# Decoder block on one core: a third column pair's first two MLP products moved to the entry of the stage, with one finished bank copied out of PSUM

## The chip, the cores and the metric

The kernel runs on one core of a Trainium2 chip. The metric is the device time of one execution, in microseconds; the time before is the median of three runs. The engines are named as in the profile: PE is TensorE's matmul, PEld its weight load, DVE is VectorE, ACT is ScalarE, POOL is GpSimd, SP is the engine that issues most of the DMAs.

## The reference

One decoder block over 1024 tokens of width 1024 in float32. Only its last part bears on the change:

```python
x = x + g1[:, None, :] * token_mixer(h, ...)          # retention + dilated attention
h = modulate(rms_norm(x, norm2_g[l]), sh2, sc2)
x = x + g2[:, None, :] * squared_relu_mlp(h, w_ff1[l], w_ff2[l])
return rms_norm(x, norm_f_g)

def squared_relu_mlp(h, w1, w2):
    return jnp.square(jax.nn.relu(h @ w1)) @ w2        # w1: 1024 x 4096, w2: 4096 x 1024
```

## The kernel before

Everything is kept transposed: 128 features on the partitions, tokens along the free dimension. Each float32 operand is split into a high part (`hi`, rounded to the format that PE multiplies) and a low part (`lo` = value minus `hi`), and each product is three matmuls, low weight by high data, high by low, high by high (`mm3`, L207, L209 and L211). The split takes two engines: ACT casts the `hi`, and then DVE subtracts to get the `lo`.

The first MLP product `h @ w1` is the function `ff1`. It works on one pair of 128-column blocks of `w1` at a time: `q` is the number of the pair, 0 to 15. For each pair the two columns by two halves of the tokens are computed with seven block products instead of eight (Winograd's form of Strassen's scheme). The products are named "11", "s1", "s3", "s2", "12", "22", "s4" (`ORDER`). Each is 4 contraction blocks of 3 matmuls of 128x512, that is 12 matmuls. "11" and "12" need only `h` of the first half of the tokens, "22" and "s4" need the second half or a sum of it, and "s1", "s3", "s2" need sums over both halves, which are called t1, t3 and t2 here (`OPERAND`).

The class `Blocks` holds the scheme. `prep` makes a weight operand: for the "s" products a DVE sum into a buffer shared by the pair (L249), then the ACT cast (L254), while the DVE subtraction for the low part (L264) is put off until the next `prep`, or until `flush` is called. `mm` issues the 12 matmuls. `post` combines finished banks on DVE and ACT. A pair has four PSUM banks: bank 0 collects "11" and then "12", bank 1 "s1" and later "s4", bank 2 "s2", bank 3 "s3" and later "22". So `post(q, "11")` copies bank 0 to SBUF before "12" is added to it (L286), and `post(q, "s2")` has DVE read bank 2 (L290) and bank 3 (L291) before "22" may be added to bank 3, and bank 1 (L1988) before "s4" may. `BANK` and `ORDER` put "12" between "s2" and "22". `run` goes through a list of items; after each product it issues the `prep` calls for which there are weight slots, then the `post`; for "s2" the `post` comes ahead of the `prep` calls. Every engine takes its instructions in the order in which this Python code issues them.

The entry of `ff1` is written out by hand. At its start the second half of the tokens isn't normalised yet: its sum of squares has just been finished by the stage before (`wo_step`). The entry runs "11" of pairs 0 and 1 around the row sums (L364) and the broadcast of the reciprocal root (L380, `n21rb`), then "12" of pairs 0 and 1. Meanwhile DVE normalises the second half (`norm`, L2038), makes t1 (L2056), t3 (L2070), t2 (L2079) and t4 (L2096), and `x_split` casts them on ACT (L2026, L2029) and subtracts on DVE (L2027, L2030). Then come "s1", "s3", "s2" of pairs 0 and 1 by hand, and `run` takes over with "s4" and "22" of both and then all products of pairs 2 to 15. There are eight PSUM banks of one tile each, so in the entry only two pairs have all their banks.

The queue of ACT in the entry is: copy of bank 0 of pair 0, copy of bank 0 of pair 1 (L286), the cast of pair 2's "s3" weight (L254), the four casts of t1, and so on. The queue of DVE is: the sums for pair 2's "s1" and "s3" weights with the low part of "s1", then the first `norm`.

`f_temps` gives the two SBUF temporaries of a pair in `post`, tags `nsq` and `h2t`, two buffers each; `norm_acc` shares `nsq` for its squares, in the stage before and in the last stage. `a_sums` makes and stores operand sums of the MLP's second product from finished pairs, at places set by `late`.

## Time and profile before

| | |
|---|---|
| median of three runs | 2219.44 us (2218.9 to 2220.44) |
| profiled execution, its own time | 2219.0 us |
| span of that execution in the profile | 2217.1 us |
| mean granted TensorE clock | 0.998 |
| PE busy | 2175.5 us, 98% of the span |
| DVE, ACT, POOL busy | 1458.5 us (66%), 919.4 us (41%), 160.8 us (7%) |
| `ff1` starts | 1569.56 us after the span's start |

A row of the timeline has the start in us from the span's start, the duration in us, engine, line of the kernel, operation, output and inputs by the program's names, and in brackets the idle time of the engine just before it with what ended it. Matmuls are pipelined: a row's duration is longer than the distance to the next one, so the pace of PE is read from the starts. A row of the waits has the total in us, how often, and the longest. A row of the windows has the length of the stretch, then the busy time and the number of instructions of each engine, then the granted clock, the DMA share and GB/s.

### The profile page before, as it was taken

What the parts mean: (1) busy time and instruction counts of PE and PEld (TensorE: products, weight loads), DVE (VectorE), ACT (ScalarE), POOL (GpSimd) and SP (SyncE); (2) the same over time, 40 slices, a digit from 0 to 9 for tenths busy, and PEclk for the clock granted to TensorE, in tenths of its full rate; (3) what the DMA queues carried; (4) which work ended last, traced back from release to release, by engine and by line L of the source; (5) the groups of instructions that cost most, each with busy time, mean ns of one, the idle gap of its engine ahead of it and who ended that gap; (6) DMA issues with size and microseconds to landing.
All of it is one profiled execution on the core that took longest, in us unless ns stands there. A gap on an engine that the chain in (4) does not pass through costs nothing. (4 is left out here: it accounts for less than half of the span.)

```text
span 2217.1 us, 27237 instructions
## 1 busy us (share of the span) xinstructions
PE 2175.5 (98%) x10130; PEld 1802.5 (81%) x10130; DVE 1458.5 (66%) x2289; ACT 919.4 (41%) x1681; POOL 160.8 (7%) x192
## 2 busy tenths in 40 slices
PE   7999999999999999999999999999999999999998
PEld 5888888888887888888888878888778888788887
DVE  6618777764548788865655654676876665787855
ACT  4323332223434544544644633524454445533412
POOL 0001111000012211111100000001100000000003
PEclk9999999999999999999999999999999999999999
DMA  9539999625775556557763265654144444745322
GB/s 365 201 133 285 298 287 287 199 105 180 249 270 185 184 189 199 178 183 196 168 173 97 68 238 190 237 179 161 65 155 154 148 147 183 253 135 173 121 86 77
DMA packets 156611, 408.93 MB, mean 184 GB/s; under 512 B 27446, under 2 KB 55357, under 8 KB 153278
## 3 DMA queue, kind: packets, MB, share of 16 engines
q1 hardware_dynamic: 148542, 363.14, 46.6%
q0 software_dynamic: 7936, 44.05, 9.0%
q8 instruction: 80, 1.31, 0.2%
q14 instruction: 53, 0.43, 0.1%
HBM read 316.27 MB, written 156.13 MB: 213 GB/s over the span
## 5 line engine op out<-in xcount | busy, mean ns | idle before, releaser
L207 PE MATMUL qap<-hh,qaw 128*128 128x512 f32 x216 | 84.0, 389 | 0.0
L209 PE MATMUL qap<-hl,qaw 128*128 128x512 f32 x216 | 84.0, 389 | 0.0
L211 PE MATMUL qap<-hh,qaw 128*128 128x512 f32 x216 | 84.0, 389 | 0.0
L631 POOL TENSOR_TENSOR j<-qk,j 128x512 fp32r<-128x512 f32 x32 | 43.3, 1352 | 459.8 <-ACT j L630 459.8
L1989 ACT ACTIVATE a<-a 128x512 f32<-128x512 f32 x48 | 30.3, 632 | 76.2 <-DVE a L1988 76.2
L1886 POOL TENSOR_TENSOR accnf<-accnf,sqnf 128x256 f32<-128x256 f32 (+1 forms) x18 | 16.6, 922 | 613.9 <-ACT sqnf L1885 613.9
L264 DVE TENSOR_TENSOR fw<-w1r,fw 128x512 fp32r<-128x512 f32 x48 | 33.0, 688 | 37.6 <-ACT fw L254 37.6
L1312 ACT ACTIVATE P<-P,ng 128x128 f32<-128x128 f32 (+1 forms) x96 | 41.9, 438 | 37.1 <-DVE ng L1309 37.1
L264 DVE TENSOR_TENSOR qaw<-wa,qaw 128x512 fp32r<-128x512 f32 x54 | 36.0, 686 | 30.8 <-ACT qaw L254 30.7
L2175 ACT CAST w2h<-w2s 128x512 fp32r<-128x512 f32 x36 | 22.4, 622 | 77.3 <-DVE w2s L2213 75.5
L207 PE MATMUL fp<-h2h,fw 128*128 128x512 f32 x128 | 50.0, 390 | 0.0
L211 PE MATMUL fp<-h2h,fw 128*128 128x512 f32 x128 | 49.8, 389 | 0.0
L207 PE MATMUL roa<-rh,rwl 128*128 128x512 f32 x128 | 49.8, 389 | 0.0
L209 PE MATMUL roa<-rl,rwh 128*128 128x512 f32 x128 | 49.8, 389 | 0.0
L211 PE MATMUL roa<-rh,rwh 128*128 128x512 f32 x128 | 49.8, 389 | 0.0
L209 PE MATMUL fp<-h2l,fw 128*128 128x512 f32 x128 | 49.8, 389 | 0.0
L1724 DVE TENSOR_TENSOR rwl<-rwl,rwh 128x1024 fp32r<-128x1024 f32 x25 | 30.2, 1220 | 29.0 <-ACT rwh L1754 29.0
L207 PEld LDWEIGHTS qap<-hh,qaw 128*128 128x128 f32 x216 | 40.5, 188 | 8.5
L666 ACT COPY sm<-sT 128x128 f32<-128x128 f32 x32 | 8.5, 267 | 93.8 <-PE sT L654 93.8
L211 PEld LDWEIGHTS qap<-hh,qaw 128*128 128x128 f32 x216 | 40.5, 188 | 8.4
L209 PEld LDWEIGHTS qap<-hl,qaw 128*128 128x128 f32 x216 | 40.5, 188 | 8.4
L1886 POOL TENSOR_TENSOR accn<-accn,sqn 128x512 f32<-128x512 f32 x12 | 15.5, 1296 | 399.9 <-ACT sqn L1885 399.9
(3097 smaller groups left out, 7210.9 us busy)
## 6 DMA issues: line engine op xcount, KB each, us to landing
v<-vd SPq DMA_DIRECT2D x32, 512.0 KB, 5.0
raw<-in_w_ada_dram SPq DMA_DIRECT2D x32, 512.0 KB, 5.0
w1r<-in_w_ff_dram SPq DMA_DIRECT2D x32, 512.0 KB, 5.0
vd<-vo SPq DMA_DIRECT2D x24, 512.0 KB, 6.3
yt<-y POOLq DMA_DIRECT2D x24, 512.0 KB, 7.3
xsd<-as SPq DMA_DIRECT2D x24, 512.0 KB, 2.8
w2r<-in_w_ff2s_dram SPq DMA_DIRECT2D x24, 512.0 KB, 7.1
em<-in_w_ada_dram SPq DMA_DIRECT2D x16, 512.0 KB, 10.2
```

Source lines behind the costliest of these rows:

```text
L207: nc.tensor.matmul(o, wl, xh, start=first, stop=False, skip_group_check=skip)
L209: nc.tensor.matmul(o, wh, xl, start=False, stop=False, skip_group_check=skip)
L211: nc.tensor.matmul(o, wh, xh, start=False, stop=last, skip_group_check=skip)
L264: nc.vector.tensor_sub(t[:, 512:], src, fv(t[:, :512]))
L631: nc.gpsimd.tensor_sub(t[:, 1], src, fv(t[:, 0]))
L666: nc.scalar.copy(sm, ps[:, :C])
L1312: nc.scalar.activation(v, v, AF.Exp, bias=ng[:, blk:blk + 1], accum_out=st[:, g, blk, 2 + a:3 + a])
L1724: nc.vector.tensor_sub(lo, fv(lo), fv(hi))
L1886: (nc.vector if f == 7 else nc.gpsimd).tensor_add(G["acc", key], G["acc", key], sq)
L1989: nc.scalar.activation(o, o, AF.Relu)
L2175: nc.scalar.copy(hi, src)
```

## The change

Pair 2's "11" now runs in the entry between "12" of pair 1 and "s1" of pair 0, with its `post`, and pair 2's "12" runs between "s1" of pair 1 and "s3" of pair 0. Both are taken out of the list that `run` gets, and `post(2, "12")` is issued after pair 2's "s3". For this, pair 2 needs a ninth bank: bank 0 of pair 0, finished after "12", is copied by ACT to a new SBUF tile `f11`, from which `post(0, "12")` reads later. The "12" weight of pair 2 is prepared in the entry too, directly behind the "s3" weight. The temporaries of `post` are given one at a time, the second only at "s2", and `nsq` has a third buffer. Two of the `a_sums` calls move to other items.

```diff
@@ Blocks.post
             if n == "11":
-                self.t[q] = self.temps(f"{self.name}t{q}")
+                self.t[q] = [self.temps(f"{self.name}t{q}", 0)]
                 nc.scalar.copy(self.t[q][0], a)
                 return
-            u, v = self.t[q]
+            if n == "s2":
+                self.t[q].append(self.temps(f"{self.name}t{q}", 1))
+            u, v = self.t[q][0], self.t[q][-1]
@@ norm_acc
-            sq = pool.tile([P, 512], F32, tag="nsq", bufs=2, name=f"sq{key}{f}")[:, :n]
+            sq = pool.tile([P, 512], F32, tag="nsq", bufs=3, name=f"sq{key}{f}")[:, :n]
@@
-    def f_temps(name):
-        return [G["mp"].tile([P, 512], F32, tag=t, bufs=2, name=name + t) for t in ("nsq", "h2t")]
+    def f_temps(name, i):
+        t = ("nsq", "h2t")[i]
+        return G["mp"].tile([P, 512], F32, tag=t, bufs=3 - i, name=name + t)
@@ ff1
         BF.mm(1, "11", range(2, 4))
         BF.post(1, "11")
-        BF.prep((2, "s3"))
+        BF.prep((2, "s3"), (2, "12"))
         BF.mm(0, "12")
+
+        t = G["mp"].tile([P, 512], F32, tag="f11", name="f11")
+        nc.scalar.copy(t, BF.ps[0][0])
+        BF.ps[0][0] = t
         BF.mm(1, "12")
...
         norm(1)
         low()
+        BF.mm(2, "11")
+        BF.post(2, "11")
         BF.mm(0, "s1")
         BF.mm(1, "s1")
+        BF.mm(2, "12")
...
-        sums = [(q, n) for q in range(2, NQ) for n in ORDER]
+        sums = [(q, n) for q in range(2, NQ) for n in ORDER if (q, n) not in ((2, "11"), (2, "12"))]
         items = [(q, n) for n in ("s4", "22") for q in range(2)] + sums
...
-        late = {(0, "22"): (0, 0), (2, "11"): (0, 1), (2, "12"): (1, 0), (2, "22"): (1, 1)}
+        late = {(0, "22"): (0, 0), (2, "s1"): (0, 1), (2, "s2"): (1, 0), (2, "22"): (1, 1)}
...
             if (q, n) in late:
                 a_sums(*late[q, n])
+            if (q, n) == (2, "s3"):
+                BF.post(2, "12")
...
-        BF.run(items, sums[3:], before, after, ("s2",))
+        BF.run(items, sums[2:], before, after, ("s2",))
```

The temporaries of the earlier scheme (`a_temps`, the attention and gate projections) follow the new form of `post` and give the same two halves of one tile as before.

More of the change, by code (lines that the diff above doesn't have):

```diff
@@ L944, in a_two, with a_temps @@
         return t.rearrange("p (a b) -> p a b", a=2)
-    def a_temps(name):
-        t = a_two(name)
-        return t[:, 0], t[:, 1]
+    pairs = {}
+    def a_temps(name, i):
+        if i == 0:
+            pairs[name] = a_two(name)
+        return pairs[name][:, i]
     def a_out(q, n, x, y=None):
```

## The prediction

> **What bounds the kernel now.** First the head of the page and the table of engines: is there one engine whose work is the span?

> ```profile
> span 2217.1 us, 27237 instructions
> PE 2175.5 (98%) x10130; PEld 1802.5 (81%) x10130; DVE 1458.5 (66%) x2289; ACT 919.4 (41%) x1681; POOL 160.8 (7%) x192
> ```

> PE is, and the change leaves the number of its matmuls as it is. It can win time only where PE waits, so the second view is PE's waits.

> ```profile
> PE n10rb L380 <- POOL n1rs L373: 8.2, 1, 8.2
> PE av L804 <- ACT hh L481: 3.6, 5, 1.2
> PE fp L209 <- DVE xt L2027: 3.6, 4, 1.1
> PE pc L418 <- DMA crow<-in_c_dram: 2.3, 1, 2.3
> PE ao L207 <- ACT g L1636: 1.8, 1, 1.8
> PE nf2ss L364 <- DVE accnf L1886: 1.6, 1, 1.6
> PE fp L207 <- DVE ft2h2t L291: 1.5, 1, 1.5
> ```

> The rows of `n10rb`, `av` and `pc` are the start of the kernel, `nf2ss` is its end. The rows of `fp` are the banks of the first MLP product: 3.6 us for low parts of t3 and t2, and 1.5 us once for a `post`. Together 5.1 us, 0.23% of the time, is all that a reordering here can take away. The rest of the argument is read from the timeline. 0.2% of 2219.44 us, 4.4 us, is about what a measurement of this kernel can tell from no change.

> First PE in the entry. A product is 12 matmuls; the first rows of products:

> ```profile
> 1580.54 0.39 PE L207 MATMUL fp<-h2h,fw 128*128 128x512 f32 x1
> ...
> 1583.26 0.39 PE L207 MATMUL fp<-xt10h,fw0s 128*128 128x512 f32 x1
> ...
> 1594.57 0.50 PE L209 MATMUL fp<-xt,fw0s 128*128 128x512 f32 x1 [1.09 <-DVE xt L2027]
> ...
> 1597.92 0.39 PE L207 MATMUL fp<-xt,fw0s 128*128 128x512 f32 x1
> ```

> These are the starts of "12" of pair 1 and "s1" of pair 0, the matmul in "s3" of pair 0 that waits last, and the start of "s2" of pair 0. A product without a wait takes 1583.26 - 1580.54 = 2.72 us. From 1583.26 to 1597.92 are four products, "s1" and "s3" of both pairs: 10.88 us of work in 14.66. The rest is "s3" of pair 0, whose matmuls come no faster than DVE makes t3. So in the entry DVE sets the pace, and the question is what the change does to DVE's queue and what to PE's.

> **The change part by part.**

> *The two products that move.* 2 x 2.72 = 5.44 us of PE work enter the stretch between "12" of pair 1 and "s3" of pair 0, and leave the run of pair 2 behind it. No matmul is added.

> *The weight for "12" of pair 2.* Its cast on ACT and its subtraction on DVE move from behind t4 to the entry. By that the subtraction for the "s3" weight moves too: `prep` flushes the one before it. In the built order of the changed kernel DVE has this subtraction directly ahead of the first `norm`, and it waits for the cast on ACT.

> ```profile
> 1573.83 0.68 DVE L249 TENSOR_TENSOR fs<-w1r,w1r 128x512 f32<-128x512 f32 x1
> ...
> 1576.64 0.75 DVE L2038 SCALAR_TENSOR_TENSOR x<-x,a,n21rb 128x512 f32<-128x512 f32 x1 [1.53 <-PE n21rb L380]
> ...
> 1579.73 0.70 DVE L2027 TENSOR_TENSOR xt10l<-x,xt10h 128x512 fp32r<-128x512 f32 x1 [0.24 <-ACT xt10h L2026]
> 1580.34 0.74 DVE L2038 SCALAR_TENSOR_TENSOR x<-x,a,n21rb 128x512 f32<-128x512 f32 x1
> ...
> 1584.97 0.69 DVE L2027 TENSOR_TENSOR xt13l<-x,xt13h 128x512 fp32r<-128x512 f32 x1
> 1585.58 0.75 DVE L2070 SCALAR_TENSOR_TENSOR x<-x,dsh,x 128x512 f32<-128x512 f32 x1
> ...
> 1578.07 0.59 ACT L286 COPY ft1nsq<-fp 128x512 f32<-128x512 f32 x1 [3.46 <-PE fp L211]
> 1578.56 0.62 ACT L254 CAST fw2s<-fs 128x512 fp32r<-128x512 f32 x1
> 1579.08 0.62 ACT L2026 CAST xt10h<-x 128x512 fp32r<-128x512 f32 x1
> ```

> The sum for "s3" is there at 1574.5 (1573.83 + 0.68), but the cast on ACT starts only at 1578.56, since ACT stands before it in the copy of pair 1's bank, which waits for PE to end that product. The cast ends at 1579.18. DVE, which starts `norm` at 1576.64 now, would be held until 1579.21 and be through at 1579.81 (a subtraction takes 0.61 from start to start, 1579.73 to 1580.34; I use 0.60): `norm` comes 3.17 us later, and behind it in DVE's queue stands everything that PE waits for: t1, t3, t2, t4. A little comes back: the 0.24 us for which t1's first subtraction waits (row 1579.73) is gone, and the cast that it waits for, which stands behind others now (1579.08), follows its sum at once; the rest of t1 is 2.85 us late. Then the flush of the "12" weight itself stands between t1 and t3 (ahead of row 1585.58), 0.60 more. **t3, t2 and t4 are 3.45 us late.**

> *The copy of the finished bank.* One ACT copy of 0.59 us (row 1578.07), behind the casts. It waits for the end of "12" of pair 0, about 1580.7, and stands ahead of t1's first cast, which now comes at 1579.08. By itself it would delay that to 1581.3; but t1's sum, 3.17 us late, ends at 1581.28. So it costs nothing, as long as DVE is the later one. The later activation reads SBUF instead of PSUM: taken as equal. The copy of pair 2's bank (0.59 us) falls in a gap of ACT before a cast that needs `norm`. The third `nsq` buffer and the two moved `a_sums` add no instruction.

> *PE in the entry.* "11" of pair 2 runs from 1583.26 to 1585.98; its weight is made ahead of all these rows already now. "s1" then finds t1's last low part at 1584.97 + 2.85 + 0.69 = 1588.51 and waits 0.3 us; both "s1" end at 1591.87, "12" of pair 2 at 1594.59. "s3" of pair 0 has no wait for its second and third block any more, but the last low part of t3, which released row 1594.57, comes 3.45 later: 1598.02. From there "s2" starts at 1597.92 + 3.45 = 1601.37. **At "s2" PE is 3.45 us late with 5.44 us of work done ahead: 1.99 us gained.** "s2" itself waits for t2 as before, 3.45 later, and so does what follows up to the end of "22" of pair 1.

> *What stands behind "s2" of pair 2.* Here is the loss. Rows of PE, then DVE:

> ```profile
> 1616.15 0.39 PE L207 MATMUL fp<-h2h,fw 128*128 128x512 f32 x1
> ...
> 1631.41 0.50 PE L207 MATMUL fp<-xt,fw 128*128 128x512 f32 x1 [1.50 <-DVE ft2h2t L291]
> ...
> 1611.06 0.69 DVE L249 TENSOR_TENSOR fs<-fs,w1r 128x512 f32<-128x512 f32 x1
> ...
> 1613.47 0.69 DVE L264 TENSOR_TENSOR fw2s<-fs,fw2s 128x512 fp32r<-128x512 f32 x1 [1.12 <-ACT fw2s L254]
> ...
> 1618.42 0.69 DVE L264 TENSOR_TENSOR fw<-w1r,fw 128x512 fp32r<-128x512 f32 x1 [2.46 <-ACT fw L254]
> ...
> 1622.38 0.69 DVE L264 TENSOR_TENSOR fw2s<-fs,fw2s 128x512 fp32r<-128x512 f32 x1 [0.74 <-ACT fw2s L254]
> ...
> 1625.55 0.69 DVE L264 TENSOR_TENSOR fw<-w1r,fw 128x512 fp32r<-128x512 f32 x1 [1.87 <-ACT fw L254]
> ...
> 1628.74 0.69 DVE L264 TENSOR_TENSOR fw3s<-fs,fw3s 128x512 fp32r<-128x512 f32 x1 [0.69 <-ACT fw3s L254]
> ...
> 1629.95 0.68 DVE L290 TENSOR_TENSOR ft2nsq<-ft2nsq,fp 128x512 f32<-128x512 f32 x1
> 1630.66 0.69 DVE L291 TENSOR_TENSOR ft2h2t<-fp,ft2nsq 128x512 f32<-128x512 f32 x1
> ```

> Now pair 2 runs from 1616.15 ("11"), and its "22" (row 1631.41) waits 1.50 us for `ft2h2t`, the read of bank 3 in the `post` of "s2", though the product "12" lies between "s2" and "22". In the changed kernel that cover is gone: "22" follows "s2" at once. PE starts pair 2's "s1" at 1616.15 + 3.45 = 1619.60 and is ready for "22" three products later, at 1627.76. And DVE? Between the first sum behind t4 (1611.06) and the `post` (1629.95) it now runs 19 instructions in 18.89 us, of which the waits for ACT take 1.12 + 2.46 + 0.74 + 1.87 + 0.69 = 6.88 (the bracketed rows). In the built order of the changed kernel there are 19 as well: weights for "s2", "s4" and "22" of pair 2, the posts of "s4" and "22" of pairs 0 and 1, three weights of pair 3, two pairs of `a_sums`. PE has 5.44 us less to do ahead of the `post`, DVE has as much. The waits change a little. The first is 1.12 + 0.60, as the subtraction of "s3" no longer fills it. The one behind the "s4" sum is 0.74 - 0.60, as the subtraction of "22" fills it. Then 2.46 and 0.69 as now. The last is 1.87 - 0.60, since it is the same way over three ACT instructions with one more DVE sum beside it. That is 6.28 in place of 6.88; and 0.11 more, as the "s4" sum has to wait for the end of the subtraction before it (like 1629.95 to 1630.66, 0.71 in place of 0.60): 18.4 us. The `post` starts at 1611.06 + 3.45 + 18.4 = 1632.9, 2.96 later than now, and PE starts "22" at 1631.41 + 2.96 = 1634.37, 6.61 us after it was ready; now it is ready at 1616.15 + 5 x 2.72 = 1629.75, 1.66 before. From "22" of pair 2 on, the work is the same in both kernels, and as the second view has no other long wait of `fp`, the delay is carried to the end. **So the sum is +2.96 us: 1.99 gained, and 6.61 - 1.66 = 4.95 lost at "22".**

> *The clock.* A wait of 6.6 us inside dense work doesn't occur in this trace; the longest between start and end is the 1.8 of `ao`. The nearest rows are two windows at the end of the kernel (the third number from the right is the granted clock) and matmuls at its start, with the same kind of matmul in the entry below them:

> ```profile
> 2206.70:2211.00 4.30, 1.32 (x8) 1.04 (x8) 2.18 (x7) 0.42 (x1) 1.44 (x2) 1.00 0.27 89
> 2211.10:2211.20 0.10, 0.00 (x0) 0.00 (x0) 0.10 (x1) 0.00 (x0) 0.00 (x0) 0.50 1.02 348
> ...
> 19.40 2.08 PE L380 MATMUL n10rb<-ct,n1rs 128*128 128x128 f32 x8 [8.24 <-POOL n1rs L373]
> 21.27 1.92 PE L380 MATMUL n11rb<-ct,n1rs 128*128 128x128 f32 x8
> 23.07 1.20 PE L804 MATMUL av<-raw_308h,hh 128*128 128x512 f32 x4
> ...
> 1575.44 1.16 PE L380 MATMUL n21rb<-ct,n21rs 128*128 128x128 f32 x8
> 1576.35 0.47 PE L207 MATMUL fp<-h2h,fw 128*128 128x512 f32 x1
> ```

> After the last product, with 1.32 us of PE work in 4.3 us, the granted clock falls to 0.50. And after the 8.2 us wait at the start, 16 broadcast matmuls take 23.07 - 19.40 = 3.67 us, while 8 take 0.91 at 1575.44: 1.82 for 16, half the time; the next products run at full pace. (The record says 1.00 there; the starts say otherwise.) So I expect the pause to drop the clock and the restart to cost 3.67 - 1.82 = 1.85 us. The bounds are 0 (no drop) and 3.3 (half pace for as long as the pause); I take 1.85, the one restart that the trace shows. [...]

> The forecast is +2.96 + 1.85 = +4.81 us. Against the profiled execution's own 2219.0 us this is 2223.8; that execution is 0.4 below the median, so on the median 2219.44 + 4.81 = **2224.2 us**.

> **The rivals.**

> *No drop of the clock.* The pause is there, the pace after it is full: +2.96, 2222.4 us. For it: no row shows a drop inside dense work. Against it: the drop at 2211 came after less idling. Chance 0.14.

> *A long restart.* The clock stays low for as long as the pause, 6.6 us, and costs 3.3: +6.3, 2225.7 us. The one restart seen, 3.67 us, speaks against it; that its length depends on when the pause falls can't be read here. Chance 0.13.

> *Faster: the moved products fill the waits.* If DVE isn't held ahead of `norm`, and the `post` of pair 2's "s2" comes when PE is ready, the 5.1 us of waits go: 2214.3 us. It decides by one point: DVE must start that `post` by 1626.3 (1627.76 less the two steps to `ft2h2t`'s end, 1.4), 6.6 us before my walk. It would need another order in DVE's queue than the built one, or casts of ACT that aren't where the trace has them. Chance 0.08.

> That the change doesn't do what it says can be left out: the built order has the 24 matmuls, the copy and the third pair's casts where the text says.

> **How the numbers follow.** The forecast has 0.65, the rivals 0.14, 0.13 and 0.08. The range reaches from the case without a drop, with the walk half a microsecond shorter, +2.4, to the long restart with the walk half a microsecond longer, +6.8: 2221.8 to 2226.3. It leaves out the faster case and some of the edges. The bound for slower is 2223.9. In the forecast's case that needs a restart of over 1.5 us, to which I give three in four: 0.49, and 0.13 from the long restart: slower 0.62. Within 0.2% are the rest of that case, 0.16, the case without a drop, 0.14, and some of the faster one, 0.02: 0.32. Faster: 0.06.

> **What would show it.** Right: DVE's first `norm` of the second half starts 3.2 us later behind a subtraction `fw2s`; "s3" of pair 0 waits once, not three times; one wait of about 6.6 us of PE at "22" of pair 2, released by `ft2h2t`; a granted clock of 0.50 in the rows behind it, with matmuls twice as far apart. Wrong: `norm` at 1576.6 still, a wait at "22" of 2 us or less, or a clock at 1.00 behind a wait of 6 us (then 2222.4).

## The result and the profile after

| | median | spread | against before |
|---|---|---|---|
| before, beside it | 2220.06 us (13 executions) | 2218.63 to 2221.33 | |
| after | 2223.90 us (13 executions) | 2221.25 to 2227.69 | 1.0020 [1.0012, 1.0027] |

The change costs 3.84 us. The profiled execution of the changed kernel is the longest of its 13, 2227.69 us, so its span stands 3.8 us above what the median would show. The head of its page and the engines:

```profile
span 2225.8 us, 27235 instructions
PE 2179.4 (98%) x10130; PEld 1806.3 (81%) x10130; DVE 1458.3 (66%) x2289; ACT 919.5 (41%) x1682; POOL 160.7 (7%) x192
```

PE has the same 10130 matmuls, and its busy time has grown by 3.9 us: matmuls have become slower somewhere. The waits of PE (total, how often, the longest):

```profile
PE n10rb L382 <- POOL n1rs L375: 9.3, 1, 9.3
PE fp L207 <- DVE ft2h2t L293: 6.8, 1, 6.8
PE fp L209 <- DVE xt L2033: 2.1, 2, 1.1
```

The waits for low parts have gone from 3.6 us to 2.1, and the one wait at "22" from 1.5 to 6.8. Together they are 3.8 us longer. The wait of `n10rb` is at the start of the kernel, ahead of everything that the change touches.

The timeline tells the same in order. PE's first matmul of `ff1`, the first two instructions of DVE behind its hold, and the only wait of PE in the "s3" of pair 0 and the one in "s2":

```profile
1572.21 0.39 PE L207 MATMUL fp<-h2h,fw 128*128 128x512 f32 x1
...
1581.88 0.69 DVE L264 TENSOR_TENSOR fw2s<-fs,fw2s 128x512 fp32r<-128x512 f32 x1 [4.11 <-ACT fw2s L254]
1582.49 0.74 DVE L2044 SCALAR_TENSOR_TENSOR x<-x,a,n21rb 128x512 f32<-128x512 f32 x1
...
1600.70 0.50 PE L209 MATMUL fp<-xt,fw0s 128*128 128x512 f32 x1 [0.99 <-DVE xt L2033]
1606.86 0.51 PE L209 MATMUL fp<-xt,fw0s 128*128 128x512 f32 x1 [1.09 <-DVE xt L2033]
```

`ff1` itself starts 2.65 us later here (1572.21 against 1569.56). The instructions of the change don't explain that: nine more profiles below have the same instructions up to that point, and in them it lies between 1569.05 and 1571.76. The profile of the changed kernel has one more fall of the granted clock ahead of it than that of before, to 0.50 from 1141.3 for 3.41 us. So everything is counted from this first matmul. DVE waits 4.11 us for ACT's cast of the weight, and `norm` starts at 10.28 instead of 7.08.

DVE ahead of the `post` of pair 2's "s2", then PE at the end of "s2" and the beginning of "22":

```profile
1617.13 0.69 DVE L249 TENSOR_TENSOR fs<-fs,w1r 128x512 f32<-128x512 f32 x1
...
1619.57 0.69 DVE L264 TENSOR_TENSOR fw2s<-fs,fw2s 128x512 fp32r<-128x512 f32 x1 [1.76 <-ACT fw2s L254]
...
1622.01 0.69 DVE L264 TENSOR_TENSOR fw2s<-fs,fw2s 128x512 fp32r<-128x512 f32 x1 [0.42 <-ACT fw2s L254]
1626.36 0.69 DVE L264 TENSOR_TENSOR fw<-w1r,fw 128x512 fp32r<-128x512 f32 x1 [2.46 <-ACT fw L254]
...
1630.32 0.69 DVE L264 TENSOR_TENSOR fw3s<-fs,fw3s 128x512 fp32r<-128x512 f32 x1 [0.74 <-ACT fw3s L254]
...
1633.48 0.69 DVE L264 TENSOR_TENSOR fw3s<-fs,fw3s 128x512 fp32r<-128x512 f32 x1 [1.27 <-ACT fw3s L254]
...
1635.89 0.68 DVE L292 TENSOR_TENSOR ft2nsq<-ft2nsq,fp 128x512 f32<-128x512 f32 x1
1636.61 0.69 DVE L293 TENSOR_TENSOR ft2h2t<-fp,ft2nsq 128x512 f32<-128x512 f32 x1
...
1630.13 0.39 PE L211 MATMUL fp<-xt,fw2s 128*128 128x512 f32 x1
1637.35 0.79 PE L207 MATMUL fp<-xt,fw 128*128 128x512 f32 x1 [6.83 <-DVE ft2h2t L293]
1637.94 0.63 PE L209 MATMUL fp<-xt,fw 128*128 128x512 f32 x1
1638.37 0.63 PE L211 MATMUL fp<-xt,fw 128*128 128x512 f32 x1
...
1643.06 0.41 PE L209 MATMUL fp<-x220l,fw2s 128*128 128x512 f32 x1
1643.32 0.39 PE L211 MATMUL fp<-x220h,fw2s 128*128 128x512 f32 x1
```

DVE's queue is unbroken from the sum at 1617.13 to the `post` at 1635.89 except for its waits for ACT, and PE stands. When it goes on, its matmuls start 0.43 us apart until 1643.06; behind that they are back at the usual 0.227 (2.72 / 12). The windows around it (length; busy time of PE, PEld, DVE, ACT, POOL; then the granted clock) show why:

```profile
1630.00:1632.00 2.00, 0.52 (x3) 0.10 (x1) 1.68 (x3) 0.64 (x2) 0.00 (x0) 1.00 1.02 378
1632.00:1634.00 2.00, 0.00 (x0) 0.00 (x0) 0.73 (x2) 1.41 (x3) 0.00 (x0) 0.71 0.42 154
1634.00:1635.00 1.00, 0.00 (x0) 0.00 (x0) 1.00 (x3) 0.00 (x0) 0.00 (x0) 0.50 1.02 385
...
1639.00:1642.00 3.00, 3.00 (x8) 2.32 (x8) 2.08 (x4) 1.37 (x3) 0.00 (x0) 0.50 0.00 0
1642.00:1644.00 2.00, 2.00 (x7) 1.55 (x7) 1.63 (x3) 0.40 (x1) 0.00 (x0) 0.73 0.61 227
```

The clock falls within the pause and returns only some 5.7 us after PE has begun again. "22" and the start of "s4" run at half pace.

### The profile page after: what moved, and what is told of

The parts are those of the page before. It is cut to its first block, busy times and chain, and to the rows that moved or that the text cites. A ratio compares the mean times of both kernels' runs of the same rounds, so it can differ in the third digit from the quotient of the medians.

```text
span 2225.8 us, 27235 instructions
## 1 busy us (share of the span) xinstructions
PE 2179.4 (98%) x10130; PEld 1806.3 (81%) x10130; DVE 1458.3 (66%) x2289; ACT 919.5 (41%) x1682; POOL 160.7 (7%) x192
## 5 line engine op out<-in xcount | busy, mean ns | idle before, releaser
L207 PE MATMUL qap<-hh,qaw 128*128 128x512 f32 x216 | 84.0, 389 | 0.0
L209 PE MATMUL qap<-hl,qaw 128*128 128x512 f32 x216 | 84.0, 389 | 0.0
L211 PE MATMUL qap<-hh,qaw 128*128 128x512 f32 x216 | 84.0, 389 | 0.0
L264 DVE TENSOR_TENSOR fw<-w1r,fw 128x512 fp32r<-128x512 f32 x48 | 33.0, 688 | 36.9 <-ACT fw L254 36.9
L264 DVE TENSOR_TENSOR qaw<-wa,qaw 128x512 fp32r<-128x512 f32 x54 | 36.0, 685 | 29.9 <-ACT qaw L254 29.9
L207 PE MATMUL fp<-h2h,fw 128*128 128x512 f32 x128 | 50.0, 391 | 0.0
L211 PE MATMUL fp<-h2h,fw 128*128 128x512 f32 x128 | 49.8, 389 | 0.0
L209 PE MATMUL fp<-h2l,fw 128*128 128x512 f32 x128 | 49.8, 389 | 0.0
L207 PE MATMUL roa<-rh,rwl 128*128 128x512 f32 x128 | 49.8, 389 | 0.0
L209 PE MATMUL roa<-rl,rwh 128*128 128x512 f32 x128 | 49.8, 389 | 0.0
L211 PE MATMUL roa<-rh,rwh 128*128 128x512 f32 x128 | 49.8, 389 | 0.0
L207 PEld LDWEIGHTS qap<-hh,qaw 128*128 128x128 f32 x216 | 40.5, 188 | 8.4
L209 PEld LDWEIGHTS qap<-hl,qaw 128*128 128x128 f32 x216 | 40.6, 188 | 8.4
L211 PEld LDWEIGHTS qap<-hh,qaw 128*128 128x128 f32 x216 | 40.6, 188 | 8.3
```

The costliest lines, as they stand in the source:

```text
L207: nc.tensor.matmul(o, wl, xh, start=first, stop=False, skip_group_check=skip)
L209: nc.tensor.matmul(o, wh, xl, start=False, stop=False, skip_group_check=skip)
L211: nc.tensor.matmul(o, wh, xh, start=False, stop=last, skip_group_check=skip)
L264: nc.vector.tensor_sub(t[:, 512:], src, fv(t[:, :512]))
```

## The experiments

Every kernel was run beside the kernel before on one chip. The table has the result, and from each profile the start of pair 2's "22" and of the last matmul of the first MLP product, both counted from that product's first matmul. The columns from the profile don't contain what happens earlier in the kernel.

| kernel | "22" of pair 2 starts | waits there | last matmul | median against before, us | ratio |
|---|---|---|---|---|---|
| before | 61.85 | 1.50 | 315.29 | | |
| after | 65.14 | 6.83 | 321.22 | +3.84 | 1.0020 [1.0012, 1.0027] |
| after, again | 65.13 | 6.84 | 321.35 | +5.95 | 1.0027 [1.0017, 1.0038] |
| filled | 65.13 | 0.50 | 318.89 | +3.10 | 1.0016 [1.0007, 1.0025] |
| filled, again | 65.14 | 0.45 | 318.01 | +3.26 | 1.0014 [1.0005, 1.0023] |
| hold alone | 65.58 | 0.87 | 318.67 | +2.45 | 1.0011 [1.0003, 1.0020] |
| no hold | 62.88 | 6.84 | 318.18 | +2.73 | 1.0017 [1.0008, 1.0026] |
| only "11" | 61.87 | 2.09 | 314.96 | -0.92 | 0.9997 [0.9988, 1.0006] |
| only "11", copy later | 60.00 | 2.11 | 314.50 | +0.02 | 0.9999 [0.9990, 1.0008] |
| only "11", spread | 58.13 | 0.26 | 311.91 | -3.23 | 0.9983 [0.9975, 0.9992] |
| the same and "12" | 61.04 | 4.99 | 316.23 | +0.49 | 1.0003 [0.9994, 1.0011] |
| later weights | 59.93 | 1.63 | 315.69 | +2.24 | 1.0011 [1.0002, 1.0020] |

**Is it the clock? The pause filled.** The changed kernel, with PE kept busy where it would stand:

```diff
@@ after(q, n), against the changed kernel
+            if (q, n) == (2, "s2"):
+                ps = ps_s("fill")
+                t, _ = BF.w[2, "s2"]
+                for i in range(28):
+                    nc.tensor.matmul(ps, t[:, :P], X["t2", 0][0], start=i == 0, stop=i == 27)
```

> The changed kernel, with 28 more matmuls of 128x512 between pair 2's "s2" and "22", into a spare bank that nothing reads (added work, 28 x 0.2265 = 6.3 us), so that PE works through most of its wait. Theory (DVE's queue sets the start of "22", and the clock falls in the pause): "22" starts where it does in the changed kernel, 65.1 us after the first matmul of the entry, at full pace; the 2.7 us of slow matmuls behind it are gone; granted clock 1.00 there; time about +3.0 to +3.3 over before less nothing else, that is 0.5 to 2.7 us under the changed kernel in like runs, and a narrower spread of its runs. Rival (the slow matmuls have nothing to do with the pause, or the fill delays "22"): the time stays at +3.8 or rises towards +10.

It was run twice, the second time beside the changed kernel itself:

> The changed kernel with 28 extra matmuls into an unused bank behind pair 2's "s2", which keep PE busy while it would wait (their results are not used). Theory: the start of "22" stays where it is, +3.0 to +3.3 us against before, at full pace. If the restart costs 1.85 us or more in the median, this is faster than the changed kernel by as much; if the fall is rare or cheap, the two agree within 1 us and the whole loss is the walk's.

> The changed kernel itself, beside its filled version on one chip, to measure what the fall of the clock costs in the median. Theory: the walk gives +3.0 to +3.3 us against before, and the restart behind the pause at pair 2's "22" adds 1.85 us by the prediction (2.6 us in the one profile of it), so the filled version is 1.8 to 2.6 us faster than this one. Rival: the fall comes only in some executions or costs less, and the two differ by less than 1 us in the median, with single executions of this kernel up to 3 us above the others.

The restart in the profile of the first filled run:

```profile
1634.18 0.50 PE L207 MATMUL fp<-xt,fw 128*128 128x512 f32 x1 [0.50 <-DVE ft2h2t L293]
1634.51 0.40 PE L209 MATMUL fp<-xt,fw 128*128 128x512 f32 x1
```

"22" starts at the same place (65.13 and 65.14 after the first matmul), as it must, since DVE is what it waits for, and it runs at full pace at once. So the place of "22" is set by DVE's queue and the pace behind it by PE's idleness; the two costs are separate. In the profiles the slow stretch takes 5.71 us for 13 steps where the filled kernel takes 0.33 + 12 x 0.227 = 3.05: 2.66 us (the second profile of the changed kernel: 6.14 us for 14 steps, 2.86 lost). Between the medians it is 2.69 us on the one chip where both ran (2225.66 against 2222.97), and 0.92 us between the first runs, which were on different chips. All executions of both pooled give 2.0 us, with a 95% interval of 0.8 to 3.9 from resampling. So the restart's cost in the median is real and of the predicted size, but known only to a microsecond or two. The single executions also spread less, as expected: by 5.0 and 4.4 us filled, by 6.4 and 5.8 us not filled.

**The hold alone.** The kernel before, with nothing but the "12" weight of pair 2 made in the entry:

```diff
@@ ff1, against the kernel before
-        BF.prep((2, "s3"))
+        BF.prep((2, "s3"), (2, "12"))
...
         norm(1)
         low()
+        BF.flush()
...
-        BF.run(items, sums[3:], before, after, ("s2",))
+        BF.run(items, [s for s in sums[3:] if s != (2, "12")], before, after, ("s2",))
```

> The kernel before, with nothing moved but the preparation of pair 2's "12" weight: its cast goes behind that of "s3" in the entry, so that DVE has the subtraction for "s3" ahead of the first norm and the one for "12" ahead of t3. Theory (DVE's queue in the entry sets t1, t3 and t2): norm 3.2 us later, "s1" of pair 0 now waits two or three times as "s3" does, t3 and t2 3.45 us later, pair 2's "22" some 2.8 us later, as two subtractions have left the queue ahead of its post; no pause over 2 us, clock 1.00; time +2.8. Rival (PE's missing cover at "22" alone makes the loss, the entry has slack): +0.5 or less.

It loses 2.45 us, near what was expected: without moved products, a `norm` held behind the cast is a plain loss. But "22" starts at 65.58, 0.9 us later than the walk gave, and the reason is in the entry, where a clock of 1.00 was expected. "s1" waits three times for t1 (0.96, 1.03 and 0.29 us). Then come PE's waits for t3, the matmuls behind them, and DVE's first read of "s2":

```profile
1592.61 0.50 PE L209 MATMUL fp<-xt,fw0s 128*128 128x512 f32 x1 [0.98 <-DVE xt L2027]
1594.66 0.51 PE L209 MATMUL fp<-xt,fw0s 128*128 128x512 f32 x1 [1.08 <-DVE xt L2027]
1596.71 0.80 PE L209 MATMUL fp<-xt,fw0s 128*128 128x512 f32 x1 [0.77 <-DVE xt L2027]
1597.31 0.63 PE L211 MATMUL fp<-xt,fw0s 128*128 128x512 f32 x1
1597.73 0.63 PE L207 MATMUL fp<-xt,fw1s 128*128 128x512 f32 x1
...
1601.98 0.40 PE L209 MATMUL fp<-xt,fw1s 128*128 128x512 f32 x1
...
1605.36 0.69 DVE L290 TENSOR_TENSOR ft0nsq<-ft0nsq,fp 128x512 f32<-128x512 f32 x1 [1.05 <-PE fp L211]
```

The clock fell here, too, with no wait longer than 1.1 us: the windows show 0.50 from 1595.13 to 1601.95, behind the waits of 0.98 and 1.08. Here it cost time: DVE waits 1.05 us for the end of "s2", where it waits 0.16 in the kernel before, and that is the 0.9.

**The hold taken away.** The changed kernel, with the "12" weight and the copy of the finished bank behind t1's casts instead of ahead of them:

```diff
@@ ff1, against the changed kernel
-        BF.prep((2, "s3"), (2, "12"))
+        BF.prep((2, "s3"))
         BF.mm(0, "12")
-        t = ... f11 ...; nc.scalar.copy(t, BF.ps[0][0]); BF.ps[0][0] = t
...
         norm(1)
         low()
+        BF.prep((2, "12"))
+        t = ... f11 ...; nc.scalar.copy(t, BF.ps[0][0]); BF.ps[0][0] = t
```

> The changed kernel without the hold in the entry: the preparation of pair 2's "12" weight and the copy of the finished bank stand behind the four casts of t1 instead of ahead of them. Theory: norm starts where it does in the kernel before, t3 and t2 come 1.2 us late instead of 3.45, "s3" of pair 0 no longer waits, and pair 2's "22" starts 2.2 us earlier than in the changed kernel; but its wait stays at 6.6 us, as PE and DVE both get there earlier, so the clock falls all the same: time 2.2 us under the changed kernel, about +1.6 over before. Rival (the wait at "22" is the loss and the hold only a part of it): the wait shrinks by the 2.2 us or more.

"22" comes 2.26 us earlier than in the changed kernel, as expected, and the whole is still 2.73 us slower than before, where 1.6 was expected. The reason is again at "22":

```profile
1632.89 0.79 PE L207 MATMUL fp<-xt,fw 128*128 128x512 f32 x1 [6.84 <-DVE ft2h2t L293]
1633.48 0.63 PE L209 MATMUL fp<-xt,fw 128*128 128x512 f32 x1
```

The hold moves PE's arrival at "22" and DVE's `post` by the same amount, so taking it away leaves the pause and its restart: "22" still starts 1.03 us later than in the kernel before, and 11 steps behind it take 4.82 us, 2.2 more than at full pace.

**The cover put back.** The changed kernel with "12" of pair 2, its weight and its `post` behind "s2" again; only "11" stays in the entry:

```diff
@@ ff1, against the changed kernel
-        BF.prep((2, "s3"), (2, "12"))
+        BF.prep((2, "s3"))
...
-        BF.mm(2, "12")
...
-... if (q, n) not in ((2, "11"), (2, "12"))]
+... if (q, n) != (2, "11")]
...
-            if (q, n) == (2, "s3"):
-                BF.post(2, "12")
```

> The changed kernel with only "11" of pair 2 in the entry; "12" and its weight are back behind "s2". Theory: "22" has its cover again and waits about 2.2 us instead of 6.8; too short for the clock to fall; the copy of the finished bank, now ahead of t1's casts without the hold, makes t1 about 1.5 us late, which eats part of what "11" fills; "22" starts within 0.3 us of where it does in the kernel before, and the time is within 0.5 us of before. Rival (a bank copied out and a third pair in the entry cost by themselves): +2 or more.

The loss is gone: 0.9997 [0.9988, 1.0006], not to be told from no change; "22" starts where it does in the kernel before, and its wait is 2.09 us. Nothing is won either, because "22" still starts when DVE's `post` lets it, and DVE comes to that `post` no earlier than before. That is two things that happen to cancel. DVE waits 2.39 us for t1's first cast, which now stands behind the copy of the bank, so its stretch ahead of the `post` starts 2.17 us later. The stretch then takes 16.74 us instead of 18.89, with the same 19 instructions but 4.82 us of waits for ACT instead of 6.88.

**DVE's queue shortened.** If that is so, then "11" in the entry gains as soon as DVE comes to that `post` earlier. Two edits to the last kernel: the copy of the bank behind t1's casts, and no weights of pair 3 prepared behind "22" of pair 1 and "s1" of pair 2 (three of them come together behind "s3" of pair 2, still ahead of the `post`). The first alone, then both:

```diff
@@ ff1, against "only 11"
-        t = ... f11 ...; nc.scalar.copy(t, BF.ps[0][0]); BF.ps[0][0] = t
         BF.mm(1, "12")
...
         norm(1)
         low()
+        t = ... f11 ...; nc.scalar.copy(t, BF.ps[0][0]); BF.ps[0][0] = t
```

> Only "11" of pair 2 moved, the copy of the finished bank behind t1's casts, pair 3's weights prepared at the places that they have in the kernel before. It parts the two edits of the spread preparation. Theory: the 2.72 us of "11" gain only as far as the post of pair 2's "s2" comes earlier: 1.7 us below before by the walk, with a wait of 1.7 to 2.1 us left at pair 2's "22". Rival (the copy's place is of no account): 0.9 us below before, as with "11" alone and the copy ahead of t1's casts.

```diff
@@ ff1, on top of it
+        now = {}
+        def rate(q):
+            return 0 if (q, now["n"]) in ((1, "22"), (2, "s1")) else 9
         def before(q, n):
+            now["n"] = n
...
-        BF.run(items, sums[2:], before, after, ("s2",))
+        BF.run(items, sums[2:], before, after, ("s2",), rate)
```

> Only "11" of pair 2 goes into the entry, with the copy of the finished bank behind t1's casts, "12" stays behind "s2" as the cover of the post, and no weights of pair 3 are prepared behind "22" of pair 1 and "s1" of pair 2, so that fewer DVE instructions stand ahead of that post. Theory (the products moved into the entry gain what they fill, and the loss is DVE's queue ahead of the post): the wait at pair 2's "22" is under 0.5 us, and the time is 3.6 us below before, about 2216.3. Rival (the entry is bound by DVE and its clock, nothing is to be gained there): about 0.9 us below before, as with "11" alone, or no change.

Both edits together are the best of all: 0.9983 [0.9975, 0.9992], 3.23 us below before, and 9.2 below the changed kernel on the same chip (2216.48 against 2225.66). PE's waits for `fp` in it:

```profile
1595.05 0.50 PE L209 MATMUL fp<-xt,fw0s 128*128 128x512 f32 x1 [1.00 <-DVE xt L2033]
1601.21 0.50 PE L209 MATMUL fp<-xt,fw0s 128*128 128x512 f32 x1 [1.08 <-DVE xt L2033]
1627.84 0.50 PE L207 MATMUL fp<-xt,fw 128*128 128x512 f32 x1 [0.26 <-DVE ft2h2t L293]
```

"22" starts 3.72 us earlier than before after a wait of 0.26, and no row behind it is slow. The number of DVE instructions ahead of the `post` is not what changed: it is 19 with the first edit alone and 19 with both. What went are two waits for ACT's casts, 1.83 of the 1.86 us by which the stretch is shorter (14.90 against 16.76). The two rows with the first edit alone, then the row directly ahead of the `post` with both:

```profile
1623.54 0.69 DVE L264 TENSOR_TENSOR fw<-w1r,fw 128x512 fp32r<-128x512 f32 x1 [0.55 <-ACT fw L254]
...
1626.70 0.69 DVE L264 TENSOR_TENSOR fw3s<-fs,fw3s 128x512 fp32r<-128x512 f32 x1 [1.28 <-ACT fw3s L254]
```

```profile
1625.78 0.69 DVE L264 TENSOR_TENSOR fw3s<-fs,fw3s 128x512 fp32r<-128x512 f32 x1
```

With the first edit alone "22" comes 1.85 us earlier, as the walk gave (1.7). The median is that of before, but its interval reaches from 2.2 us below to 1.8 above, so it decides neither for the 1.7 nor for the rival's 0.9. In the profile, most of the gain is spent right behind "22":

```profile
1630.58 0.50 PE L207 MATMUL fp<-xt,fw 128*128 128x512 f32 x1 [2.11 <-DVE ft2h2t L293]
...
1631.38 0.62 PE L207 MATMUL fp<-xt,fw 128*128 128x512 f32 x1
...
1634.78 0.40 PE L211 MATMUL fp<-xt,fw 128*128 128x512 f32 x1
```

Eight steps of 0.43, 3.40 us, are 1.59 us more than at full pace, behind a pause of 2.11 us. In the kernel "only 11" a pause of 2.09 at the same place had no slow stretch behind it.

**The cover taken away from the best kernel.** The best kernel with "12" moved to the entry, its weight behind t1's casts so that nothing holds `norm`:

```diff
@@ ff1, on top of "only 11, spread"
+        BF.prep((2, "12"))
...
         BF.mm(1, "s1")
+        BF.mm(2, "12")
...
-... if (q, n) != (2, "11")]
+... if (q, n) not in ((2, "11"), (2, "12"))]
...
+            if (q, n) == (2, "s3"):
+                BF.post(2, "12")
```

> The kernel of the spread preparation with one thing more: "12" of pair 2 runs in the entry too (its weight made behind t1's casts, so that nothing holds the first norm), and "22" follows "s2" of pair 2 at once. Theory (the product "12" is worth more behind "s2" than in the entry): a wait of 4.7 us at pair 2's "22" comes back; by the walk 1.1 us below before at full pace, 2.4 above the kernel without this move, and, if that pause drops the clock too, 0.5 to 1.5 us above before. Rival (the loss was only the hold ahead of norm and the early weights of pair 3): no more than 0.5 us above the kernel without the move, about 3 us below before.

The medians differ by 2220.38 - 2216.48 = 3.9 us (on two chips, whose runs of before have medians of 2219.89 and 2219.71). Expected were 2.4 at full pace and, with a fall of the clock, 0.5 to 1.5 above before, which is 3.7 to 4.7 above the best kernel; the rival's 0.5 is out. A pause of 5 us is back, and the clock falls:

```profile
1629.00:1631.00 2.00, 0.39 (x1) 0.39 (x2) 1.93 (x4) 1.46 (x3) 0.00 (x0) 0.90 0.79 290
1631.00:1633.00 2.00, 2.00 (x6) 1.52 (x6) 0.88 (x2) 1.66 (x3) 0.00 (x0) 0.50 0.00 0
```

So with the hold gone and the stretch shortened, moving "12" is still what takes the gain away. The profiles say how, and it isn't by PE's cover alone: "22" starts 2.91 us later than in the best kernel because DVE's `post` does. DVE's stretch starts 0.88 later and takes 16.93 us instead of 14.90, with 19 instructions again. "Only 11, copy later" and "no hold" differ by the same move of "12", without the spread, and by the same 0.88 and 2.00. Then comes the restart: 8 steps in 3.50 us, 1.6 more than at full pace. Why DVE waits longer for ACT with "12" moved wasn't tried.

**Weights of pair 3 later, in the changed kernel.** The second edit above, with "s3" of pair 2 as a third place without weights, and the hold and "12" as in the changed kernel:

```diff
@@ ff1, against the changed kernel
+            return 0 if (q, now["n"]) in ((1, "22"), (2, "s1"), (2, "s3")) else 9
...
-        BF.run(items, sums[2:], before, after, ("s2",))
+        BF.run(items, sums[2:], before, after, ("s2",), rate)
```

> The changed kernel with pair 3's weights not prepared behind "22" of pair 1, "s1" and "s3" of pair 2: they come behind the post of "s2". Theory (DVE has a fixed amount of work up to pair 3's "22" and is late by it): the wait at pair 2's "22" shrinks to under 2 us, but a new wait of about 3.8 us appears at pair 3's "22", and the sum is +2.0 us against before. Rival (only the order ahead of the one post is at fault): the wait goes without another in its place, and the time is 1 to 2 us below before.

```profile
1630.94 0.50 PE L207 MATMUL fp<-xt,fw 128*128 128x512 f32 x1 [1.63 <-DVE ft2h2t L293]
1652.37 0.50 PE L207 MATMUL fp<-xt,fw 128*128 128x512 f32 x1 [2.08 <-DVE ft3h2t L293]
```

The wait at pair 2's "22" shrinks and another appears at pair 3's, and the time, +2.24 us, is the theory's and not the rival's. The new wait is smaller than expected, 2.08 for 3.8, and in this profile the last matmul comes only 0.40 us later than before. The profiled execution is one of the shortest of this kernel (2220.91; the median is 2221.95). How the 2.24 us of the median come about isn't settled by it.

## Why the prediction was right

The mechanism is as predicted, and the sum of +4.81 lies between the two measurements of the changed kernel, +3.84 and +5.95. That the median of 2223.9 is only 0.3 us from the forecast is partly luck: the kernel before ran 0.6 us slower beside it than in the three runs that the forecast starts from, and the difference is 1.0 smaller than forecast, while in the profile both terms are larger, 3.29 and 2.66, in sum 5.95. Its steps, one by one, counted from the first matmul of `ff1`:

- *The hold of DVE ahead of `norm`.* 3.20 us later behind `fw2s` (10.28 against 7.08); predicted 3.17.
- *The entry.* "s3" of pair 0 waits once and not three times, and the wait in "s2", for a low part of t2, ends at 34.65 instead of 31.17: 3.48 later, predicted 3.45.
- *DVE's stretch ahead of the `post`.* It starts 3.42 us later (1617.13 and 1611.06, each from its start) and takes 18.76 us, where 18.4 was predicted. The waits for ACT are 1.76, 0.42, 2.46, 0.74 and 1.27, in sum 6.65 for 6.28. This term was mis-sized by 0.37, most of it in the second wait: 0.42, not 0.14. The subtraction that was to fill that wait shortens it from 0.74 by 0.32, not by 0.60.
- *"22" of pair 2.* It starts 3.29 us later, predicted 2.96; the 0.33 between them is that mis-sized term. The pause is 6.83 in the profile, predicted 6.6.
- *The clock.* It falls to 0.50 and matmuls start at 0.43 instead of 0.227, as predicted. The restart costs 2.66 us in the profile where 1.85 was taken, within the bounds of 0 and 3.3; between the medians of the changed and the filled kernel it is 0.9 and 2.7. The row from the start of the kernel, two groups of broadcast matmuls, was a fair price for the median and too low for the two profiles of the changed kernel. It wasn't the only restart in the trace of before, and "no row shows a drop inside dense work" overlooked one: behind the 1.85 us wait of `ao`, in the stage of the attention output, the clock falls for 3.41 us, which at half pace is an estimated 1.7 us:

```profile
1286.07:1289.48 3.41, 3.41 (x10) 2.67 (x9) 0.88 (x1) 0.00 (x0) 0.00 (x0) 0.50 1.00 363
```

Of the rivals, "no drop of the clock" is out: in all four profiles with a pause of 4.99 us or more (the changed kernel twice, "no hold", and the best kernel with "12" moved) the clock fell. The "long restart" isn't out: 2.66 and 2.86 in the profiles are nearer to its 3.3 than to 1.85, and of the two medians +3.84 is nearer to the forecast and +5.95 to its +6.3. The faster rival named its condition correctly: the gain comes when DVE starts that `post` early enough, by 1626.3 or 56.7 us after the first matmul. "Only 11, spread" starts it at 56.67, and wins 3.23 of the 5.1 us of waits; the changed kernel starts it at 63.68.

In three of these four profiles the granted clock is at 0.50 for 3.41 us (the best kernel with "12") and for 10.24 (the changed kernel, twice), of which 3.4 to 6.2 us lie behind the start of "22"; 10.24 is three times 3.41. What sets the length wasn't tried; the last section has where the changes of the clock lie in two profiles.

## What to carry to other kernels

Before a product is moved to fill one wait, look at what it covers where it stands: here "12" was the 2.72 us of PE work between "s2" and "22", while DVE's `post` frees the bank of "22". With "12" moved and that `post` later, PE stood for 6.8 us. When PE waits for a release by DVE, PE's order can't win anything until DVE comes to that release earlier; so look at what the move does to DVE's queue, its waits for ACT as much as its instructions. "11" moved, with two such waits taken out of the queue, won 3.23 us. How much of that the second edit would win without "11" moved wasn't run. A pause of PE in dense work is priced with its restart, here 1.6 to 2.9 us in four profiles on top of the pause.

## What the hardware showed unexpectedly

The granted clock fell not only in pauses of 5 us and more. It fell behind two waits of 0.98 and 1.08 us ("hold alone"), in the entry of "only 11" behind two waits of 1.08, and behind one pause of 2.11 ("only 11, copy later"); it didn't fall in the entry of before, behind waits of 0.38, 1.07 and 1.09, nor behind a pause of 2.09 ("only 11"). The last pair of pauses stands at the same place and differs by 0.02 us.

```profile
1594.20:1597.61 3.41, 1.37 (x5) 0.48 (x3) 3.34 (x7) 1.83 (x3) 0.00 (x0) 1.00 0.00 0
1597.61:1601.02 3.41, 3.28 (x8) 2.61 (x9) 3.34 (x6) 0.75 (x2) 0.00 (x0) 0.50 0.00 0
...
1628.33:1631.74 3.41, 2.02 (x9) 1.32 (x8) 3.14 (x6) 0.79 (x2) 0.00 (x0) 1.00 0.59 219
1631.74:1635.15 3.41, 2.71 (x12) 2.25 (x13) 2.71 (x5) 2.01 (x5) 0.00 (x0) 1.00 0.30 112
```

And the pair of "only 11, copy later" around the pause of 2.11:

```profile
1627.96:1631.37 3.41, 1.30 (x6) 0.76 (x5) 3.34 (x7) 0.71 (x2) 0.00 (x0) 1.00 0.55 208
1631.37:1634.78 3.41, 3.41 (x9) 2.66 (x8) 2.71 (x5) 3.35 (x7) 0.00 (x0) 0.50 0.00 0
```

PE is busy for 1.37 of 3.41 us (40%) and 1.30 (38%) ahead of the two falls. The pause of 2.09 is split between two windows and leaves 2.02 (59%) and 2.71 (79%). So nearly the same wait had a restart behind it in one profile and none in another. No run moved a wait from one window to the next with all else kept, so that its place among the windows decides this is the author's reading of these profiles and not shown.

In the entry of "only 11" the slow stretch costs next to nothing, since "22" waits for DVE behind it and DVE waits 0.24 us for the end of "s2" where it waited 0.16; in "hold alone" it cost 0.9. Such falls go with the spread of single executions, which is 4 to 6 us for most of these kernels. Of the 83 executions of the kernel before beside the experiments, those with a mean granted clock of 0.999 take 2217.8 us on average, those with 0.998 2219.4, those with 0.997 2221.2. That the falls are the whole of it wasn't tried.
